# Four moves in the first third of a fused decoder layer: a gate tile ahead of attention, channel means behind a gate group, a weight split behind a convolution input, seven weight splits on another engine

## The chip, the cores and the metric

The kernel runs on one core of one Trainium2 chip. The metric is the device time of one execution in microseconds (us); the kernel before has a median of 1292.92 us over three runs (1291.68 to 1296.99). All positions below are us from the start of the span of the profiled execution. PE is TensorE, DVE is VectorE, ACT is ScalarE, POOL is GpSimd, SP is SyncE, which here only issues DMAs.

## The reference, cut to what matters

One layer over 1040 tokens (16 meta tokens in front of 1024), width 1024, all in float32:

```python
z = h @ w_in + b_in                       # 3840 columns: q | k | v | conv value, conv gate | two merge gates
a = swa_sink_attention(q, k, v, sinks, rel_bias)      # window 128, 8 heads, 16 meta keys, sinks
y_attn = a @ w_attn_proj
c = c_val * sigmoid(c_gate)
c = causal_dwconv(c, conv_dw, conv_dw_b)              # 31 taps, 512 channels
c = silu(layer_norm(c, conv_ln_g, conv_ln_b))         # mean and variance over the 512 channels
y_conv = c @ w_conv_proj
mixed = sigmoid(g_attn) * y_attn + sigmoid(g_conv) * y_conv
h = layer_norm(alpha * h + mixed @ w_out, ...)
h = layer_norm(alpha * h + conv_ffn(h), ...)
```

## The kernel before, in words

Every product of float32 matrices is made of three products in a reduced type (`fp32r`): each operand is split into a high and a low part, and high x high, high x low and low x high are summed in PSUM (`product`, lines 332, 335, 336). A weight tile of 1024 x 128 is loaded by SP (`weights`), its high part is a cast on ACT (`split`, line 300), and its low part a subtraction (line 303). That subtraction runs on DVE for the first 23 weight tiles of the kernel (the argument `n <= 23`) and on POOL for later ones. Two buffers each of the raw, high and low weights are in use, so that a tile's cast waits until PE has finished the tile two before it.

The input projection is worked through in tiles of 128 output columns, each over three groups of tokens (`z_tile`, `z_group`). One tile is 3 groups x 8 blocks x 3 matmuls, and each group has one of three PSUM banks until an evacuation has read it. The order of the tiles by count is: 1 to 3 the key tile, the value tile and the first query tile; 4 and 5 the gate and the value tile of convolution chunk 1 (`conv_chunk`); 6 and 7 those of chunk 0; 8 to 10 the other query tiles; 11 and 12 merge gates 0 and 1; 13 and 14 chunk 2; 15 to 17 gates 2 to 4; 18 and 19 chunk 3; 20 to 30 gates 5 to 15. So gate i has count 15 + i from gate 5 on. Weight tiles 31 to 38 belong to the projection of the two branches.

A convolution chunk leaves its input in `cin`, through three evacuations on DVE (line 697), one for each token group. The 31 taps (line 706) follow on DVE as 31 instructions for each of the four chunks, at a low rank, so that they fill DVE's time during attention. Behind chunk 3 the four chunks are summed into `csum`, two additions on POOL and the last (line 919) on DVE, and PE multiplies `csum` by a matrix of 1/512 to get the channel means (line 924), for three token groups.

Attention goes over eight blocks of 128 queries and two key groups: scores (lines 784 and 864), softmax on DVE and ACT, transposes, weighted values. Queries go out to DRAM (`qd`) and come back in another layout (`qt`), so that the first scores wait for that transfer.

The normalisation over channels, called the chain below, runs behind attention on DVE in an order written out by hand (`pin`): `cln_centre` (line 961), `cln_var` (line 971; sums over channels by PE, line 973), `cln_rstd` (lines 979 to 982), `cln_scale` (line 989, Silu on ACT, line 990), `cln_split` (lines 996, 997), and then `o_split` (lines 1008 to 1010), which scales the attention output and splits it. The last eight `o_split` calls serve token groups 1 and 2. The branch projection (`ps_p`) reads what `cln_split` and `o_split` write. The temporaries of the chain lie where attention had its tiles.

The order of instructions on each engine is set by a planner that simulates the kernel when it is built: among the instructions that are ready in its simulation it takes the one with the lowest rank (`rank`, `tc.cur_priority`). `after(x, y)` adds an edge to it: x is ordered behind y. On the chip each engine then runs its own list in order. Ranks that matter here: 500 for weight splits, 600 for evacuations, 30000 for attention, 38000 for the chain, 40000 for gate tiles, 60000 for taps, 70000 for the projection.

Of the kernel before, what the change touches and what calls it, by code (L numbers as in the profile page):

```python
# [26 lines left out]
OP = mybir.AluOpType  # L27
# [4 lines left out]
KC = D // P  # L32
# [78 lines left out]
def tile_hybrid_layer(  # L111
# [3 lines left out]
    nc = tc.nc  # L115
# [5 lines left out]
    def load(o, i):  # L121
        return nc.sync.dma_start(out=o, in_=i)

    def store(o, i):

        return nc.scalar.dma_start(out=o, in_=i)

    def f32(ap):
        return ap.bitcast(F)

    def after(ins, first):

        tc.add_manual_dep(ins.ins, first.ins.name, mybir.DependencyInfo(
            mybir.DependencyClass.NoSync, mybir.DependencyReason.SCHED_ONLY), reason="order of work")

    @contextmanager
    def rank(p):

        saved = tc.cur_priority
        tc.cur_priority = p  # L140
        yield
        tc.cur_priority = saved
# [35 lines left out]
    start = ExitStack()  # L178
# [45 lines left out]
    def bcol(m):  # L224
        return colA[:, m:m + 1]
# [10 lines left out]
    def ones_of(pool):  # L236
        t = pool.tile([P, P], F, name="ones", tag="ones", bufs=1)
        nc.vector.memset(t, 1.0 / CW)
        return t

    ones = ones_of(sp)
# [35 lines left out]
    def h0(k, hl, a, b):  # L277
        return (RHO, RHC)[hl][:, k * T + a:k * T + b]
# [17 lines left out]
    def wraw(shape):  # L296
        return wraw_p.tile(shape, F, name="wr", tag="wr")

    def split(raw, hi, lo, quick=False, behind=None):
        ins = nc.scalar.copy(hi, raw)  # L300
        if behind is not None:
            after(ins, behind)
        return (nc.vector if quick else nc.gpsimd).tensor_tensor(lo, raw, f32(hi), OP.subtract)  # L303

    def wsp(tag, dtype=R):
        return wsp_p.tile([P, KC, WS], dtype, name=tag, tag=tag)
# [1 line left out]
    def wsp_flat(tag, dtype=R):  # L308
        return wsp(tag, dtype).rearrange("p k c -> p (k c)")[:, W_FLAT:W_FLAT + D]

    fills = [0]
    last_fill, last_split = [], []

    def weights(shape, fill):
        fills[0] += 1
        n = fills[0]
        own = n == 3
        raw = OB[:, 0:D].rearrange("p (k c) -> p k c", k=KC) if own else wraw(shape)
        with rank({1: 14, 2: 13, 3: 16, 4: 23}.get(n, RK_SPLIT)):
            last_fill.append(fill(raw))  # L320
        hi, lo = ((sp.tile([P, KC, WS], R, name=t + "3") if own else wsp(t))[:, :, :P] for t in ("whi", "wlo"))
        if n <= 3:
            return hi, lo, raw
        with rank(RK_SPLIT):
            last_split.append(split(raw, hi, lo, n <= 23))
        return hi, lo

    def product(ps, terms, behind=None):

        n = len(terms)  # L330
        for i, (ah, al, bh, bl) in enumerate(terms):
            ins = nc.tensor.matmul(ps, ah, bh, start=i == 0, stop=False)  # L332
            if i == 0 and behind is not None:
                after(ins, behind)
            nc.tensor.matmul(ps, ah, bl, start=False, stop=False)  # L335
            last = nc.tensor.matmul(ps, al, bh, start=False, stop=i == n - 1)  # L336
        return last

    def z_group(wt, g, a, b, evac):
        hi, lo = wt  # L340
        ps = pat.tile([P, 512], F, name="ps_z", tag="mm", bufs=3)
        product(ps[:, :b - a], [(hi[:, k], lo[:, k], h0(k, 0, a, b), h0(k, 1, a, b)) for k in range(KC)])
        with rank(RK_EVAC):
            evac(g, a, b, ps[:, :b - a])

    def z_tile(fill, groups, evac, wt=None):
        wt = wt or weights([P, KC, P], fill)
        for g, (a, b) in enumerate(groups):
            z_group(wt, g, a, b, evac)

    def in_cols(m):
        return lambda raw: load(raw, w_z[m])

    TG = [(a + U0 if i == 0 else a, b) for i, (a, b) in enumerate(HG)]
# [3 lines left out]
    def stage(n, lo=4104, cnt=5):  # L358
        i = st_next[0] % cnt
        st_next[0] += 1  # L360
        return FA[:, lo + i * 400:lo + i * 400 + n]
# [158 lines left out]
    def span(i, g):  # L520
        a, b = HG[g]
        return (U0 if i == 2 and g == 0 else a), b
# [21 lines left out]
    def evac(g, *tiles):  # L544
        for i in tiles:
            a, b = span(i, g)
            with rank(RK_EVAC):
                evacs0[i](g, a, b, sums0[i])
# [92 lines left out]
    for a, b in ((0, 400), (400, J_LEN)):  # L641
        ps = pat.tile([P, 512], F, name="ps_v", tag="o" if a == 0 else "t", bufs=1 if a == 0 else 2)
# [17 lines left out]
    ones = ones_of(cp)  # L660
# [4 lines left out]
    Kx = [ap.tile([P, NB, 144], R, name=f"kx{g}") for g in range(NKV)]  # L665
# [17 lines left out]
    def conv_chunk(c):  # L683
        sig = {}

        def g_evac(g, a, b, ps):
            sig[g] = stage(b - a)

            nc.scalar.activation(sig[g], ps, AF.Tanh, bias=bcol(10 + c), scale=0.5)
            nc.scalar.activation(sig[g], sig[g], AF.Identity, bias=half_, scale=0.5)  # L690

        z_tile(in_cols(10 + c), HG, g_evac, wt_c1 if c == 1 else None)
        cin = cp.tile([P, 16 + T], F, name="cin", tag="cin")
        nc.vector.memset(cin[:, 0:16], 0.0)

        def v_evac2(g, a, b, ps):
            nc.vector.scalar_tensor_tensor(cin[:, 16 + a:16 + b], ps, bcol(6 + c), sig[g], OP.add, OP.mult)  # L697

        z_tile(in_cols(6 + c), HG, v_evac2)
        with rank(RK_CONV + c * 100):  # L700
            for j in range(TAPS):
                wc = cdw[:, j * CH + c:j * CH + c + 1]
                if j == 0:
                    nc.vector.tensor_scalar(acc[c], cin[:, j:j + U], wc, cdwb(c), OP.mult, OP.add)
                else:
                    nc.vector.scalar_tensor_tensor(acc[c], cin[:, j:j + U], wc, acc[c], OP.mult, OP.add)  # L706

    def gate_tile(i):
        b2, m = divmod(i, KC)

        def gate_evac(g, a, b, ps):
            t = stage(b - a)
            nc.scalar.activation(t, ps, AF.Tanh, bias=bcol(14 + i), scale=0.5)  # L713
            store(sgd[b2, m, :, a - U0:b - U0], t)

        z_tile(in_cols(14 + i), TG, gate_evac)

    for g in range(NKV):
        kr = FA[:, 2054 + g * T:2054 + (g + 1) * T]
# [24 lines left out]
    ps = pat.tile([P, 512], F, name="ps_vm", tag="t", bufs=2)  # L744
# [4 lines left out]
    for q4 in range(2):  # L749
        ps = pat.tile([P, 512], F, name="ps_v4", tag="t", bufs=2)  # L750
        for i in range(4):
            c = NMETA + (q4 * 4 + i) * P
            nc.tensor.transpose(ps[:, i * P:(i + 1) * P], vT[:, c:c + P], ident)
        src = ps[:, :].rearrange("p (n g d) -> p n g d", g=2, d=HD)
        for g in range(NKV):
            hi, lo = (V[:, q4 * 4:q4 * 4 + 4, g, i] for i in range(2))
# [10 lines left out]
    def load_q(g, i):  # L767

        n = P if i else P + 2
        t = ap.tile([P, 8 * (P + 2)], R, name="qt", tag="qt", bufs=3)[:, :8 * n]  # L770
        for h in range(2):
            load(f32(t[h * HD:(h + 1) * HD]), dram(qd, g * HD * 8 * U + q_at(i), [[8 * U, HD], [1, 8 * n]]))
        t = t.rearrange("p (l r q) -> p l r q", l=2, r=4)
        return t[:, 0], t[:, 1]

    tc.cur_priority = RK_ATT


    q0 = [load_q(g, 0) for g in range(NKV)]
    ps = pat.tile([P, 512], F, name="ps_s2", tag="t", bufs=2)  # L780
    for h in range(NH):
        g, r = divmod(h, 4)
        o = ps[:2, h * 16:(h + 1) * 16]
        nc.tensor.matmul(o, q0[g][0][:, r, 0:2], Kx[g][:, 0, 0:16], start=True, stop=False)
        nc.tensor.matmul(o, q0[g][1][:, r, 0:2], Kx[g][:, 0, 0:16], start=False, stop=True)
    s2 = ap.tile([2, NH, 16], F, name="s2")
    nc.vector.tensor_tensor(s2, ps[:2, :P].rearrange("p (h m) -> p h m", m=16), biasq, OP.add)
# [44 lines left out]
    ps = pat.tile([P, 512], F, name="ps_o", tag="o", bufs=1)  # L832
# [16 lines left out]
    for i in range(NB):  # L849
# [5 lines left out]
        for g in range(NKV):  # L855
# [6 lines left out]
            for r in range(4):  # L862
                ps = pat.tile([P, 512], F, name="ps_s", tag="s", bufs=2)
                nc.tensor.matmul(ps[:, :w], qh[:, r], keys, start=True, stop=False)
                nc.tensor.matmul(ps[:, :w], ql[:, r], keys, start=False, stop=True)
                h = g * 4 + r
# [18 lines left out]
            for c, kb in bands:  # L885
                ps = pat.tile([P, 512], F, name="ps_t", tag="t", bufs=2)
# [17 lines left out]
            weights_out(range({2: 0, 5: 3, 7: 6}[i], i + 1))  # L904

    tc.cur_priority = RK_Z
    order = list(range(0, 2)) + ["c2"] + list(range(2, 5)) + ["c3"] + list(range(5, 16))
    for o in order:
        if isinstance(o, str):
            conv_chunk(int(o[1]))  # L910
# [2 lines left out]
        if o == "c3":  # L913

            csum = cp.tile([P, 16 + T], F, name="csum", tag="cin")[:, :U]
# [4 lines left out]
    means = {}  # L920
    for g, (a, b) in enumerate(UG):
        with rank(RK_EVAC):
            means[g] = pat.tile([P, 512], F, name="ps_m", tag="st"[g % 2], bufs=2)
            nc.tensor.matmul(means[g][:, :b - a], ones, csum[:, a:b], start=True, stop=True)
    att.close()
    qsp_stack.close()

# [9 lines left out]
    ones = ones_of(tmp_p)  # L937
# [158 lines left out]
    for m in range(KC):  # L1096
        hi, lo = weights([P, KC, P], lambda raw: load(raw, w_ab[m]))
# [37 lines left out]
        if m in (2, 3):  # L1135
            raw = (FA[:, 4112:5136], OB[:, 3072:4096])[m - 2]
# [343 lines left out]
    for c in range(FC):  # L1480
        V4, X, Z, Y = (pup.tile([P, 1024], F, name=n, tag=n) for n in ("pw", "px", "pz", "py"))
        passes = ((1,), (0,)) if c == 0 else ((0, 1),)
        for subs in passes:
            last = subs == passes[-1]
            w_next = iter(range(7))
            a, b = SUB[subs[0]][0], SUB[subs[-1]][1]
# [54 lines left out]
            ins = tt(c22[:, a:b], c22[:, a:b], u13[:, a:b], OP.add)  # L1541
# [239 lines left out]
```

## Time and profile before

| | |
|---|---|
| median of three runs | 1292.92 us (1291.68 to 1296.99) |
| the profiled execution, and its span | 1290.93 us, 1289.1 us |
| busy: PE, DVE, ACT, POOL | 98%, 84%, 45%, 5% of the span |
| mean granted TensorE clock | 0.995 |
| input projection, attention, gates on PE | up to 436.65 us |
| branch and output projection, then the up and the down stage | from 436.65 us on |

A row of the timeline or of the waits has the start, the duration, the engine, the line, the operation, the output and inputs with their shapes, a count, and in brackets the idle time before it and what ended that. A row of the windows has a stretch, its length, the busy time of each engine with the number of instructions, the granted clock (1.00 is full) and the share and rate of the DMA engines.

### The profile page before, as it was taken

What the parts mean: (1) busy time and instruction counts of PE and PEld (TensorE: products, weight loads), DVE (VectorE), ACT (ScalarE), POOL (GpSimd) and SP (SyncE); (2) the same over time, 40 slices, a digit from 0 to 9 for tenths busy, and PEclk for the clock granted to TensorE, in tenths of its full rate; (3) what the DMA queues carried; (4) which work ended last, traced back from release to release, by engine and by line L of the source; (5) the groups of instructions that cost most, each with busy time, mean ns of one, the idle gap of its engine ahead of it and who ended that gap; (6) DMA issues with size and microseconds to landing.
All of it is one profiled execution on the core that took longest, in us unless ns stands there. A gap on an engine that the chain in (4) does not pass through costs nothing.

```text
span 1289.1 us, 21679 instructions
## 1 busy us (share of the span) xinstructions
PE 1263.4 (98%) x8546; PEld 1189.8 (92%) x8546; DVE 1085.9 (84%) x1836; ACT 580.3 (45%) x1051; POOL 66.4 (5%) x35
## 2 busy tenths in 40 slices
PE   7999999999999999999999999999999999999997
PEld 7889999999989999788899999999999997888886
DVE  7888999999967777647899999989899886887697
ACT  5423234454547222344664554555545543536330
POOL 2100000001112222100000000000000000000000
PEclk9999999999999999999999999999999999999999
DMA  6274734334243665222235454453455556989722
GB/s 245 83 265 108 185 93 116 100 82 115 67 112 119 201 166 146 92 82 82 83 103 204 173 208 178 182 202 129 161 182 195 196 198 242 393 286 388 260 76 82
DMA packets 96297, 212.11 MB, mean 165 GB/s; under 512 B 11059, under 2 KB 36211, under 8 KB 95938
## 3 DMA queue, kind: packets, MB, share of 16 engines
q1 hardware_dynamic: 84426, 199.64, 46.2%
q10 hardware_dynamic: 11768, 11.08, 2.6%
q8 instruction: 67, 1.10, 0.4%
q14 instruction: 36, 0.29, 0.1%
HBM read 150.29 MB, written 62.70 MB: 165 GB/s over the span
## 4 chain that ended last, share of the span: by engine, by line
PE 80%; DVE 13%; DMA 4%; ACT 1%; issue 1%; SPq 1%; ACTq 0%; POOL 0%; DVEq 0%
PE px L1502 14%; PE py L1502 9%; PE ps_x L1627 9%; PE ps_z L1627 5%; PE ps_z L332 5%; PE ps_z L335 5%; PE ps_z L336 5%; PE pz L1502 5%; PE pw L1502 5%; DVE FA L706 4%; PE ps_p L336 2%; PE ps_p L335 2%; PE ps_p L332 2%; PE ps_w L332 2%; PE ps_w L336 2%; PE ps_w L335 2%
## 5 line engine op out<-in xcount | busy, mean ns | idle before, releaser
L332 PE MATMUL ps_z<-RHO,whi 128*128 128x384 f32 (+2 forms) x648 | 209.8, 324 | 2.6 <-DVE cin L697 2.6
L335 PE MATMUL ps_z<-RHC,whi 128*128 128x384 f32 (+2 forms) x648 | 210.1, 324 | 0.0
L336 PE MATMUL ps_z<-RHO,wlo 128*128 128x384 f32 (+2 forms) x648 | 209.5, 324 | 0.0
L706 DVE SCALAR_TENSOR_TENSOR FA<-cin,cdw,FA 128x1026 f32<-128x1026 f32 x120 | 154.9, 1305 | 0.1
L332 PEld LDWEIGHTS ps_z<-RHO,whi 128*128 128x128 f32 x648 | 122.5, 189 | 3.5 <-DVE cin L697 3.0
L336 PEld LDWEIGHTS ps_z<-RHO,wlo 128*128 128x128 f32 x648 | 122.3, 189 | 1.2 <-issue 0.3
L335 PEld LDWEIGHTS ps_z<-RHC,whi 128*128 128x128 f32 x648 | 122.6, 189 | 0.7
L300 ACT CAST whi<-wr 128x1024 fp32r<-128x1024 f32 x37 | 38.8, 1049 | 75.6 <-PE ps_z L335 58.4
L1324 DVE TENSOR_TENSOR RHO<-wr,RHO 128x512 fp32r<-128x512 f32 x94 | 64.0, 689 | 9.5 <-ACT RHO L1323 9.5
L1323 ACT CAST RHO<-wr 128x512 fp32r<-128x512 f32 x94 | 56.7, 619 | 25.8 <-DVE wr L1341 11.6
L1341 DVE TENSOR_TENSOR wr<-wr 128x512 f32<-128x512 f32 x88 | 60.6, 689 | 0.2
L303 POOL TENSOR_TENSOR wlo<-wr,whi 128x1024 fp32r<-128x1024 f32 x17 | 42.1, 2474 | 187.2 <-ACT whi L300 158.8
L1514 ACT COPY FA<-px 128x514 f32<-128x514 f32 (+2 forms) x23 | 13.1, 571 | 79.0 <-PE px L1502 79.0
L713 ACT ACTIVATE FA<-ps_z,colr 128x384 f32<-128x384 f32 (+1 forms) x48 | 26.0, 542 | 48.4 <-PE ps_z L336 46.4
L1502 PE MATMUL px<-OA,RHO 128*128 128x258 f32 x324 | 43.2, 282 | 0.0
L1429 ACT ACTIVATE FA<-OB,coll 128x512 f32<-128x512 f32 x44 | 35.9, 816 | 15.2 <-DVE OB L1510 15.2
L1502 PE MATMUL px<-OC,RHO 128*128 128x256 f32 x324 | 42.2, 280 | 0.0
L1502 PE MATMUL px<-RHC,RHO 128*128 128x258 f32 (+1 forms) x312 | 40.9, 280 | 0.4 <-ACT OB L1514 0.4
L1514 ACT COPY OB<-px 128x514 f32<-128x514 f32 (+2 forms) x46 | 26.1, 567 | 32.6 <-PE px L1502 32.6
L1502 PEld LDWEIGHTS px<-OA,RHO 128*128 128x128 f32 x324 | 40.5, 189 | 0.2 <-ACT OB L1514 0.2
L880 ACT ACTIVATE s<-s,sm 128x272 f32<-128x272 f32 (+1 forms) x64 | 31.8, 500 | 18.1 <-DVE sm L876 16.3
L1502 PEld LDWEIGHTS px<-OC,RHO 128*128 128x128 f32 x324 | 39.9, 189 | 0.1
(468 smaller groups left out, 3387.2 us busy)
## 6 DMA issues: line engine op xcount, KB each, us to landing
wr<-in_w_up_dram SPq DMA_DIRECT2D x44, 512.0 KB, 4.2
wr<-in_w_z_dram SPq DMA_DIRECT2D x29, 512.0 KB, 4.0
fd<-FA SPq DMA_DIRECT2D x44, 256.0 KB, 2.5
OB<-in_w_down_dram SPq DMA_DIRECT2D x21, 512.0 KB, 4.7
FA<-sd SPq DMA_DIRECT2D x15, 512.0 KB, 8.1
qt<-qd SPq DMA_DIRECT2D x28, 256.0 KB, 4.0
sgd<-FA ACTq DMA_DIRECT2D x32, 192.0 KB, 2.6
td<-OB SPq DMA_DIRECT2D x12, 512.0 KB, 3.2
```

Of the source, the lines that this page charges most:

```text
L300: ins = nc.scalar.copy(hi, raw)
L303: return (nc.vector if quick else nc.gpsimd).tensor_tensor(lo, raw, f32(hi), OP.subtract)
L332: ins = nc.tensor.matmul(ps, ah, bh, start=i == 0, stop=False)
L335: nc.tensor.matmul(ps, ah, bl, start=False, stop=False)
L336: last = nc.tensor.matmul(ps, al, bh, start=False, stop=i == n - 1)
L706: nc.vector.scalar_tensor_tensor(acc[c], cin[:, j:j + U], wc, acc[c], OP.mult, OP.add)
L1323: nc.scalar.copy(hi, src)
L1324: ins = nc.vector.tensor_tensor(lo, src, f32(hi), OP.subtract)
L1341: ins = nc.vector.tensor_tensor(*x)
L1502: ins = nc.tensor.matmul(o, x[:, ks], bmat(sub, q, hl, k), start=first and k + j == 0, stop=k == 3 and j == 2, skip_group_check=not first)
L1514: copied.append(nc.scalar.copy(*x))
L1627: nc.tensor.matmul(banks[i], l[:, ts], r[:, ws], start=first and a and x + k == 0, stop=z and x == len(ops) - 1 and k == 2, skip_group_che ...
```

## The change

Four edits, none of which adds or removes arithmetic:

1. Gate tile 0 is written ahead of attention instead of behind it, and attention's first matmul is ordered behind the last matmul of that tile.
2. The three channel-mean products are ordered behind the first token group of gate tile 12.
3. The low part of weight tile 7 (the value tile of chunk 0) is ordered behind the last evacuation into the convolution input of chunk 1. Both run on DVE.
4. The low parts of weight tiles 24 to 30 (gates 9 to 15) are made on DVE instead of POOL.

To name these points, `z_group` and `z_tile` return their last matmuls.

```diff
-    fills = [0]
+    fills, cin_done, gate_mm = [0], [], {}
...
-            last_split.append(split(raw, hi, lo, n <= 23))
+            last_split.append(split(raw, hi, lo, n <= 30))
+            if n == 7:
+                after(last_split[-1], cin_done[-1])
...
-        product(ps[:, :b - a], [(hi[:, k], lo[:, k], h0(k, 0, a, b), h0(k, 1, a, b)) for k in range(KC)])
+        last = product(ps[:, :b - a], [(hi[:, k], lo[:, k], h0(k, 0, a, b), h0(k, 1, a, b)) for k in range(KC)])
         with rank(RK_EVAC):
             evac(g, a, b, ps[:, :b - a])
+        return last
...
-        for g, (a, b) in enumerate(groups):
-            z_group(wt, g, a, b, evac)
+        return [z_group(wt, g, a, b, evac) for g, (a, b) in enumerate(groups)]
...
-            nc.vector.scalar_tensor_tensor(cin[:, 16 + a:16 + b], ps, bcol(6 + c), sig[g], OP.add, OP.mult)
+            cin_done.append(nc.vector.scalar_tensor_tensor(cin[:, 16 + a:16 + b], ps, bcol(6 + c), sig[g],
+                                                           OP.add, OP.mult))
...
-        z_tile(in_cols(14 + i), TG, gate_evac)
+        gate_mm[i] = z_tile(in_cols(14 + i), TG, gate_evac)
...
+    gate_tile(0)
     tc.cur_priority = RK_ATT
...
-        nc.tensor.matmul(o, q0[g][0][:, r, 0:2], Kx[g][:, 0, 0:16], start=True, stop=False)
+        ins = nc.tensor.matmul(o, q0[g][0][:, r, 0:2], Kx[g][:, 0, 0:16], start=True, stop=False)
+        if h == 0:
+            after(ins, gate_mm[0][-1])
...
-    order = list(range(0, 2)) + ["c2"] + list(range(2, 5)) + ["c3"] + list(range(5, 16))
+    order = [1, "c2"] + list(range(2, 5)) + ["c3"] + list(range(5, 16))
...
-            nc.tensor.matmul(means[g][:, :b - a], ones, csum[:, a:b], start=True, stop=True)
+            ins = nc.tensor.matmul(means[g][:, :b - a], ones, csum[:, a:b], start=True, stop=True)
+            after(ins, gate_mm[12][0])
```

## The prediction, before the run

> **What bounds the kernel now.** I read the page first: who is busy, and who makes up the chain that ended last.
>
> ```profile
> span 1289.1 us, 21679 instructions
> PE 1263.4 (98%) x8546; PEld 1189.8 (92%) x8546; DVE 1085.9 (84%) x1836; ACT 580.3 (45%) x1051; POOL 66.4 (5%) x35
> ```
>
> PE is busy for 98% of the span, so the time is PE's work plus its holes. No edit removes PE work; the change can only close holes or open new ones. So the second view is the list of waits, for PE alone.
>
> ```profile
> PE ps_z L332 <- DVE cin L697: 2.6, 1, 2.6
> PE ps_s L784 <- DMA qt<-qd: 1.5, 2, 1.1
> PE ps_m L924 <- DVE csum L919: 1.4, 1, 1.4
> ```
>
> Three of the four edits name exactly these places: tile 7's low weights the first, the gate tile the second, the means the third. The third view is the timeline around each.
>
> **Edit 3, the first hole.**
>
> ```profile
> 86.61 1.04 ACT L300 CAST whi<-wr 128x1024 fp32r<-128x1024 f32 x1 [10.62 <-PE ps_z L335]
> 87.69 1.23 DVE L303 TENSOR_TENSOR wlo<-wr,whi 128x1024 fp32r<-128x1024 f32 x1 [4.98 <-ACT whi L300]
> 88.83 1.55 DVE L697 SCALAR_TENSOR_TENSOR cin<-ps_z,colr,FA 128x272 f32<-128x272 f32 x3
> 89.38 0.59 PE L332 MATMUL ps_z<-RHO,whi 128*128 128x272 f32 x1 [2.63 <-DVE cin L697]
> 94.00 0.34 PE L332 MATMUL ps_z<-RHO,whi 128*128 128x384 f32 x1
> 62.44 0.29 PE L332 MATMUL ps_z<-RHO,whi 128*128 128x272 f32 x1
> 65.44 0.34 PE L332 MATMUL ps_z<-RHO,whi 128*128 128x384 f32 x1
> 90.00:91.00 1.00, 1.00 (x6) 1.00 (x6) 1.00 (x3) 0.00 (x0) 0.00 (x0) 0.50 0.80 266
> ```
>
> Tile 7's split stood 4.98 us at the head of DVE's queue for its cast, which waited for a buffer that PE was still reading. All three evacuations of the chunk before stood behind it, and PE needed their banks: 2.63 us of hole. The hole cost more than its length. The windows row shows the granted clock at 0.50 behind it, and the 24 matmuls from 89.38 to 94.00 took 4.62 us where the same 24 from 62.44 to 65.44 took 3.00. With the split behind the evacuations, two of these run in DVE's idle time and the third as the tile ends. The split itself then starts when its cast is done, as before, and tile 7's matmuls begin over 10 us after that (tile 6, which takes 11, comes first). Nothing else is late. Gain: 2.63 + 1.62 = 4.25 us.
>
> The Trainium skill (TensorE: Matmul & The Clock Gate, Part 1) lets the clock fall only after an idle window of about 3.4 us. By it this hole would have cost 2.63 us alone, and the sum at the end would be 1.6 us less good. The trace disagrees: 2.63 us were enough for a clock of 0.50.
>
> **Edit 1, the second hole.**
>
> ```profile
> 137.65 0.28 PE L332 MATMUL ps_z<-RHO,whi 128*128 128x258 f32 x1
> 149.09 0.28 PE L332 MATMUL ps_z<-RHO,whi 128*128 128x258 f32 x1
> 153.81 0.17 PE L784 MATMUL ps_s<-kx,qt 128*2 128x16 f32 x1 [1.14 <-DMA qt<-qd]
> 155.96 0.17 PE L784 MATMUL ps_s<-kx,qt 128*2 128x16 f32 x1 [0.37 <-DMA qt<-qd]
> ```
>
> Gate 0 already begins at 149.09, ahead of attention; the scores cut into it and wait 1.14 + 0.37 = 1.51 us for queries. A tile takes 11.44 us (137.65 to 149.09). With gate 0 whole it ends at 149.09 + 11.44 - 4.25 = 156.3, after the queries have landed, so the 1.51 us are gained. The first of the two left the clock at 1.00 (first row of the next fence), so there is nothing more. The price is that all of attention waits 2.5 us longer (153.81 to 156.3), with its softmax on DVE and ACT behind it. DVE covers that with taps:
>
> ```profile
> 105.00:155.00 50.00, 35.48 (x29) 1.00 0.55 136
> 305.00:355.00 50.00, 30.63 (x23) 1.00 0.31 94
> ```
>
> These windows hold DVE's taps alone (busy time and count, then clock); there are taps to do from 105 until past 355, and gate tiles to do on PE beyond that. Without that cover the price would be 2.5 us. I take nothing.
>
> **Edit 2, the third hole.** The means wait 1.44 us for the last sum, with everything on PE behind them. Behind gate 12's first group that wait is gone: `csum` ends at 364.07, that group 20 us later. But the means then come late for DVE's chain, whose first step they are. What counts is how long the projection can do without the chain:
>
> ```profile
> 361.11 2.96 DVE L919 TENSOR_TENSOR csum<-csum,FA 128x1026 f32<-128x1026 f32 x1
> 364.13 1.35 PE L924 MATMUL ps_m<-csum,ones 128*128 128x386 f32 x4 [1.44 <-DVE csum L919]
> 365.31 1.95 DVE L961 TENSOR_TENSOR FA<-FA,ps_m 128x386 f32<-128x386 f32 x4
> 369.86 0.81 PE L924 MATMUL ps_m<-csum,ones 128*128 128x384 f32 x2
> 379.98 2.16 DVE L971 TENSOR_TENSOR t<-t 128x386 f32<-128x386 f32 x3 [0.28 <-ACT t L970]
> 393.49 0.34 PE L332 MATMUL ps_z<-RHO,whi 128*128 128x384 f32 x1
> 432.74 0.56 DVE L1010 TENSOR_TENSOR OA<-OB,OA 128x384 fp32r<-128x384 f32 x1
> 436.65 0.28 PE L332 MATMUL ps_p<-OA,whi 128*128 128x258 f32 x1
> 440.60 0.28 PE L332 MATMUL ps_p<-OA,whi 128*128 128x256 f32 x1
> ```
>
> In the kernel before, the early means are of no use to the chain after its first step: centring runs from 365.31, but the variance waits until 379.98, since its temporaries lie on attention's tiles. The slack at the end: the last split of token group 1 is done at 433.30, and PE reads it first at 440.60 (fourth block of the projection's second group). That is 7.3 us; the other groups have more.
>
> Now the chain after. Gate 12's first group ends at 393.49 before. Take off the three holes, 4.25 + 1.51 + 1.44 = 7.20 us, and what PE did ahead of that point and now does behind it: the means (about 2.0) and two variance sums, 0.8 each by the 0.81 row. That leaves 393.49 - 7.20 - 3.6 = 382.7. The first mean takes 0.8, centring two groups 2 x 1.95, so the variance starts at 387.4 instead of 379.98: 7.4 us later by the clock, though all of PE is 7.2 earlier.
>
> **Edit 4, POOL to DVE.**
>
> ```profile
> L303 DVE TENSOR_TENSOR wlo<-wr,whi x20: 1192/1218/1226, 55.3 to 315.6; 128x1024 fp32r<-128x1024 f32 x20
> L303 POOL TENSOR_TENSOR wlo<-wr,whi x17: 2386/2406/3467, 329.8 to 533.3; 128x1024 fp32r<-128x1024 f32 x17
> 346.21 3.47 POOL L303 TENSOR_TENSOR wlo<-wr,whi 128x1024 fp32r<-128x1024 f32 x1 [14.04 <-ACT whi L300]
> 347.33 2.44 DVE L803 TENSOR_TENSOR pm<-s,pm 128x64 f32<-128x64 f32 x1
> 407.52 2.41 POOL L303 TENSOR_TENSOR wlo<-wr,whi 128x1024 fp32r<-128x1024 f32 x1 [10.93 <-ACT whi L300]
> 407.54 3.69 DVE L989 TENSOR_TENSOR FA<-FA,t 128x256 f32<-128x256 f32 x4
> 414.99 2.42 POOL L303 TENSOR_TENSOR wlo<-wr,whi 128x1024 fp32r<-128x1024 f32 x1 [5.05 <-ACT whi L300]
> 415.18 2.44 DVE L1009 CAST OA<-OB 128x386 fp32r<-128x386 f32 x1
> 418.73 0.36 DVE L1009 CAST OA<-OB 128x386 fp32r<-128x386 f32 x1
> 437.85 2.40 POOL L303 TENSOR_TENSOR wlo<-wr,whi 128x1024 fp32r<-128x1024 f32 x1 [8.87 <-ACT whi L300]
> DVE wlo L303 <- ACT whi L300: 10.7, 5, 5.0
> ```
>
> It looks like 7 x 1.22 = 8.5 us more for a DVE that has no room. But a DVE instruction that starts beside a POOL split stands until it is over: the cast at 415.18 took 2.44 us, the same cast at 418.73 took 0.36; a 128x64 subtraction took 2.44. So POOL's splits already cost DVE about 2 us where they hit. Inside the chain two go away (407.52: 3.69 for four that should take some 1.4; 414.99: 2.1), 4.4 us in all. In their place come the DVE splits of tiles 29 and 30 at 1.2 each, of which one should fall into a wait for ACT: +1.2 (ends 0 and 2.4). Each also waits for its cast at the head of DVE's queue; the nearest row for that is the 4.98 at 87.69, the other end is nothing, and I take nothing, as 5 of the 20 DVE splits waited at all (last row). The first three moved splits lie ahead of `csum`, which has 20 us of room. Last, tile 32's split stays on POOL: at 437.85 it came just behind the chain's end; PE being 7.2 earlier and the chain later, it falls inside: +2.2 (ends 0 and 2.2).
>
> The Trainium skill (Perfetto Trace Analysis, Optimizing Scalar/DVE Operations) says that moving work between GpSimd and VectorE might not help, since they share a port. By it edit 4 would be worth nothing, and the sum would be 3.2 us worse. The trace agrees on the sharing (the two casts) but gives the move a gain inside the chain.
>
> **The sum.** The chain's end moves by S = 7.4 - 4.4 + 1.2 + 2.2 = 6.4 us. PE wants it 7.2 earlier and has 7.3 of slack, so PE waits 6.4 + 7.2 - 7.3 = 6.3 us in the projection, and the net is -7.2 + 6.3 = -0.9 us. If the planner sees that wait, it can put the convolution half of the second group in front of it, 12 matmuls of 0.12 us (33 of them lie between 436.65 and 440.60), 1.4 us; PSUM has one bank for that, not more. I take it, since the planner orders by readiness: -2.3 us (ends 0 and 2.8 for this term). Against the profiled execution (1290.93, span 1289.1) that is 1288.6; its time is 2.0 below the median shown, so the median becomes 1292.9 - 2.3 = 1290.6 us.
>
> **The rivals.** *All of the gain stays.* If the chain is shorter than I think, -7.2: 1285.7 us. It has waits to give, as the window of DVE's busy time over the chain shows:
>
> ```profile
> 379.00:438.00 59.00, 48.82 (x98) 1.00 0.53 150
> ```
>
> That is 10.2 us of waiting, and over 4 us of the busy time were blocked instructions. S must fall under 0.1. For it: the planner makes a new order for ACT, on which DVE waits there. Against: DVE's pinned order stays, and ACT's work is the same.
>
> *Slower: the chain is the bound.* One mechanism: the late means. If no wait shrinks, both new splits cost DVE and one waits for its cast as at 87.69, S = 6.4 + 1.2 + 5.0 = 12.6, and the net is 12.6 - 7.3 = +5.3. If a hole reaches 2.63 us, the clock falls and adds 1.6: +6.9, 1299.8 us. It decides from S = 7.3 on.
>
> *The change does not do what it says.* Gate 0 is already first; if the planner's new order only moves the holes (its simulation put tile 7's split before its cast), the time stays at 1293.
>
> **How the numbers follow.** Most of it paid back (-5 to +2): 0.50; all kept: 0.22; slower: 0.22; holes moved: 0.06. What a measurement can tell is about 0.5%, or 6.5 us. All kept lies just beyond it, so about two thirds of it counts as faster: 0.15. Of the slower case, with orders of the planner I can't foresee, three quarters lie beyond: 0.16. The range goes from the kept gain to the slower end: 1285.5 to 1299.5; the likeliest case alone is 1288 to 1295.
>
> **What would show it.** Right: no wait on `cin`, `qt` or `csum` in PE's list; clock 1.00 from 80 to 100; gate 12's first group ends near 383, the means right behind it; variance from about 387; POOL's first split of a weight is tile 31. PE waits at the first projection group for `OA`, some 5 us in pieces. Wrong: no such wait (gain kept), one piece of over 2.6 us with the clock at 0.50, or DVE standing for a cast in front of the chain.

## The result, and the profile after

The changed kernel takes 1290.64 us (median of 20 runs, 1288.21 to 1291.79) against 1294.37 us for the kernel before on the same chip (20 runs, 1290.98 to 1296.99). The ratio is 0.9971, with an interval of 0.9963 to 0.9979: 3.7 us faster. The median forecast was 1290.6 us, from a gain of 2.3. The profiled spans are 1289.1 and 1287.0 us.

The list of waits of PE in the changed kernel, without those that both kernels have at the start and in the last stages:

```profile
PE ps_z L334 <- ACT FA L716: 2.0, 1, 2.0
PE ps_p L337 <- DVE OA L1017: 1.9, 1, 1.9
```

The three waits on `cin`, `qt` and `csum` are gone and two others have come. The second, at the projection, had been forecast in kind, but as 6.3 us less 1.4. The first had not: PE waits for a bank that ACT has not emptied (the gate's evacuation, line 716 now). These are the places on PE's timeline, the means and the first scores among them:

```profile
62.95 0.29 PE L334 MATMUL ps_z<-RHO,whi 128*128 128x272 f32 x1
156.59 0.17 PE L788 MATMUL ps_s<-kx,qt 128*2 128x16 f32 x1
381.58 1.89 PE L930 MATMUL ps_m<-csum,ones 128*128 128x386 f32 x6
414.11 0.45 PE L334 MATMUL ps_z<-RHO,whi 128*128 128x384 f32 x1 [2.01 <-ACT FA L716]
419.96 0.28 PE L334 MATMUL ps_z<-RHO,whi 128*128 128x258 f32 x1
431.39 0.28 PE L334 MATMUL ps_p<-OA,whi 128*128 128x258 f32 x1
432.12 0.28 PE L334 MATMUL ps_p<-OA,whi 128*128 128x258 f32 x1
432.24 0.28 PE L334 MATMUL ps_p<-OC,whi 128*128 128x258 f32 x1
435.49 0.39 PE L337 MATMUL ps_p<-OA,whi 128*128 128x258 f32 x1 [1.90 <-DVE OA L1017]
```

The projection starts at 431.39 instead of 436.65. Counted from the first matmul of weight tile 4 (62.95 here, 62.44 before), so that the start of each execution does not come in, it starts 5.8 us earlier. The rows at 432.12 and 432.24 show the planner's new order: the attention half (`OA`) and the convolution half (`OC`) of a group alternate. The clock, by windows, at the old hole and behind the new one (the column behind POOL's):

```profile
86.00:90.00 4.00, 4.00 (x32) 4.00 (x31) 2.42 (x4) 1.05 (x1) 0.00 (x0) 1.00 0.71 279
414.00:418.00 4.00, 3.89 (x14) 3.89 (x15) 3.83 (x9) 1.60 (x4) 0.00 (x0) 0.59 0.66 165
```

The old hole is filled. Behind the new one the clock falls to a mean of 0.59 over four microseconds, and the 24 matmuls from 414.11 to 419.96 take 5.85 us, where half of the 48 of this shape between two tiles take some 4.2 (the gate tile's 11.44 us hold 24 of 258 columns, 3.0, and 48 of 384). So this hole cost 2.0 + 1.6 us in this execution. With the 1.9 at the projection, 5.5 us are paid back.

On DVE, the chain's first and last steps and what held it up, with POOL beside it:

```profile
386.16 1.88 DVE L978 TENSOR_TENSOR t<-t 128x386 f32<-128x386 f32 x3
392.76 1.23 DVE L303 TENSOR_TENSOR wlo<-wr,whi 128x1024 fp32r<-128x1024 f32 x1 [1.60 <-ACT whi L300]
413.61 1.23 DVE L303 TENSOR_TENSOR wlo<-wr,whi 128x1024 fp32r<-128x1024 f32 x1 [3.49 <-ACT whi L300]
432.54 2.47 POOL L303 TENSOR_TENSOR wlo<-wr,whi 128x1024 fp32r<-128x1024 f32 x1 [8.47 <-ACT whi L300]
432.83 2.61 DVE L1017 TENSOR_TENSOR OA<-OB,OA 128x386 fp32r<-128x386 f32 x1
442.07 0.56 DVE L1017 TENSOR_TENSOR OA<-OB,OA 128x384 fp32r<-128x384 f32 x1
```

The variance starts at 386.16 (387.4 was forecast) and the last split of token group 1 ends at 442.63: the chain's end moved by 9.3 us, not 6.4. Both splits that fall into the chain stood for their casts, tile 29's for 1.60 us and tile 30's for 3.49. Tile 32's split on POOL held the last low part of token group 0 for 2 us, and it is this instruction that PE waited for. ACT shows why both the cast and the evacuation were late:

```profile
408.25 1.28 ACT L985 ACT_TABLE_LOAD   x1
409.55 0.47 ACT L985 ACTIVATE t<-ps_m,eps 128x256 f32<-128x256 f32 x1
410.04 1.28 ACT L997 ACT_TABLE_LOAD   x1
411.34 1.31 ACT L997 ACTIVATE FA<-FA,colr 128x384 f32<-128x384 f32 x2
412.55 1.03 ACT L300 CAST whi<-wr 128x1024 fp32r<-128x1024 f32 x1
413.49 0.57 ACT L716 ACTIVATE FA<-ps_z,colr 128x384 f32<-128x384 f32 x1
```

These six rows fill 408.25 to 414.06 without a gap. PE reaches its next group at about 412.1 and needs the bank that the last row empties. It is behind two table loads of 1.28 us, a root and two Silu steps of the chain, and the cast.

### The profile page after: what moved, and what is told of

It is laid out like the page before. It is cut to its first block, busy times and chain, and to the rows that moved or that the text cites. A ratio compares the mean times of both kernels' runs of the same rounds, so it can differ in the third digit from the quotient of the medians.

```text
span 1287.0 us, 21685 instructions
## 1 busy us (share of the span) xinstructions
PE 1263.6 (98%) x8546; PEld 1191.0 (93%) x8546; DVE 1083.7 (84%) x1843; ACT 582.9 (45%) x1053; POOL 49.8 (4%) x28
## 4 chain that ended last, share of the span: by engine, by line
PE 88%; DVE 6%; DMA 2%; ACT 2%; issue 1%; SPq 0%; POOL 0%; DVEq 0%; ACTq 0%
PE px L1509 14%; PE py L1509 9%; PE ps_x L1634 9%; PE ps_z L334 7%; PE ps_z L337 7%; PE ps_z L338 7%; PE ps_z L1634 5%; PE pz L1509 5%; PE pw L1509 5%; PE ps_w L338 2%; PE ps_w L334 2%; PE ps_w L337 2%; PE ps_p L338 2%; PE ps_p L334 2%; PE ps_p L337 2%; DVE RHC L509 1%
## 5 line engine op out<-in xcount | busy, mean ns | idle before, releaser
L303 DVE TENSOR_TENSOR wlo<-wr,whi 128x1024 fp32r<-128x1024 f32 x27 | 32.8, 1216 | 14.5 <-ACT whi L300 14.4
L1509 PEld LDWEIGHTS px<-RHC,RHO 128*128 128x128 f32 x312 | 38.5, 189 | 0.7 <-ACT OB L1521 0.7
```

The source lines that it names most:

```text
L1509: ins = nc.tensor.matmul(o, x[:, ks], bmat(sub, q, hl, k), start=first and k + j == 0, stop=k == 3 and j == 2, skip_group_check=not first)
```

## The experiments

Two questions were open. Is each edit worth what its own hole cost? And do the late means set the payback, or ACT's and DVE's order, or POOL? Twelve kernels were run: each edit alone, the changed kernel without one edit, and the means at other places. All are compared with the kernel before on the same chip, whose median was 1293.94 to 1294.86 us.

### Each edit alone

The kernel before, with edit 3 alone:

```diff
             last_split.append(split(raw, hi, lo, n <= 23))
+            if n == 7:
+                after(last_split[-1], cin_done[-1])
```

> The kernel before with edit 3 alone (tile 7's low weights behind the evacuations). My theory: the hole at 87 goes with its slow clock, 4.25 us, and all later work moves with it, since the projection had 7.3 us of slack: about -4.2 us. Rival, that a hole costs only its idle time: -2.6 us. Rival, that a new order by the planner opens another hole: 0.

1289.89 us, ratio 0.9969 (0.9958 to 0.998), some 4.0 us faster. The profiles show the same size:

```profile
64.19 0.29 PE L334 MATMUL ps_z<-RHO,whi 128*128 128x272 f32 x1
434.16 0.28 PE L334 MATMUL ps_p<-OA,whi 128*128 128x258 f32 x1
```

From the first matmul of tile 4 to the first of the projection it is 369.97 us, and 374.21 in the kernel before (62.44 to 436.65): 4.24 us less, although the wait for queries is 2.1 us here for 1.5. With edit 2 alone:

```diff
-            nc.tensor.matmul(means[g][:, :b - a], ones, csum[:, a:b], start=True, stop=True)
+            ins = nc.tensor.matmul(means[g][:, :b - a], ones, csum[:, a:b], start=True, stop=True)
+            after(ins, gate_mm[12][0])
```

> The kernel before with edit 2 alone (means behind gate 12's first group). My theory: the wait for the last sum goes (-1.44), but the chain starts some 12 us later in absolute time less the 4.6 us that it had to wait for attention anyway, its splits stay on POOL, and the projection waits: +2 to +6 us net. Rival, that the chain has idle time to give: -1.4 us.

1299.19 us, ratio 1.0038 (1.0024 to 1.0052), 4.9 us slower. Its list of waits has two new holes as in the changed kernel, for ACT and in the projection, beside the two old ones that the edit does not touch. The wait on `csum` is gone, but one of the same length in attention has come in its place:

```profile
PE ps_z L332 <- DVE cin L697: 2.6, 1, 2.6
PE ps_z L332 <- ACT FA L714: 2.0, 1, 2.0
PE ps_s L785 <- DMA qt<-qd: 1.9, 1, 1.9
PE ps_pm L809 <- DVE pl L893: 1.4, 1, 1.4
PE ps_p L332 <- DVE OA L1011: 1.2, 1, 1.2
```

So edit 2 alone is enough to bring both new holes, at lines 714 and 1011 there. With edit 4 alone:

```diff
-            last_split.append(split(raw, hi, lo, n <= 23))
+            last_split.append(split(raw, hi, lo, n <= 30))
```

> The kernel before with edit 4 alone (seven low parts on DVE). My theory: DVE gains about 1.5 us net before the sum and 3 in the chain, none of which PE can use except at the wait for the last sum, which is at most 1.4: between 0 and -1.4 us. Rival, that DVE stands for casts as at tile 7 and the last sum comes later: +1 to +4 us.

1292.09 us, ratio 0.9986 (0.9977 to 0.9995), 1.8 us faster; the wait for `csum` is gone from its list. But the wait for queries is 2.2 us there for 1.5, and a wait for ACT's gate evacuation has come:

```profile
PE ps_z L332 <- ACT FA L714: 0.9, 1, 0.9
```

So in its profiled execution PE stands no less than before, and where the 1.8 us come from is not shown. With edit 1 alone:

```diff
+    gate_tile(0)
     tc.cur_priority = RK_ATT
...
+        if h == 0:
+            after(ins, gate_mm[0][-1])
...
-    order = list(range(0, 2)) + ["c2"] + list(range(2, 5)) + ["c3"] + list(range(5, 16))
+    order = [1, "c2"] + list(range(2, 5)) + ["c3"] + list(range(5, 16))
```

> The kernel before with edit 1 alone (gate tile 0 whole, then attention). My theory: -1.5 us, the two waits for queries. Rival, that attention's later start reaches the last sum, for which PE waits: up to +2.5 us, net +1.

1292.29 us, ratio 0.9988 (0.9979 to 0.9997), 1.6 us faster, but not only by the two waits for queries. These are gone from its list, and so is the wait on `csum`, for the last sum now ends at 356.6. In their place stands a wait for ACT's gate evacuation, with the clock at 0.50 behind it:

```profile
PE ps_z L332 <- ACT FA L714: 2.4, 1, 2.4
408.00:409.00 1.00, 1.00 (x4) 1.00 (x5) 1.00 (x1) 1.00 (x3) 1.00 (x1) 0.50 0.46 169
```

The means run from 356.6 in this kernel, so this wait does not need late means. The theory held for all four in sign. Edit 3 has the size of its hole by its mechanism; that edit 1 has it too is a coincidence. Edits 1, 3 and 4 alone add up to 7.4 us, with edit 2 to 2.5.

### The changed kernel without one edit

> The changed kernel without edit 2 (means as early as the planner likes). My theory: the last sum is done at 352, so PE hardly waits for it even without edit 2, the chain starts early: 2 to 6 us faster than the changed kernel, 1284.5 to 1288.5. Rival, that edit 2 is needed for the gain: slower than the changed kernel by the 1.4 us of the old wait, 1292.

Without `after(ins, gate_mm[12][0])` the time is 1284.06 us, ratio 0.9919 (0.9906 to 0.9931): 10.5 us faster than before, and 6.7 faster than the changed kernel. The edge is not needed for the third hole. This kernel is the one before with edits 1, 3 and 4: together they are worth 10.5 us, where alone they add up to 7.4 (a difference just beyond the intervals), and the waits for ACT that edits 1 and 4 bring alone are not in its list. Edit 2 on top of them costs 6.7 us. In the changed kernel the last sum is done at 351.6, 12 us earlier than before:

```profile
L925 DVE TENSOR_TENSOR csum<-csum,FA x1: 1199/1199/1199, 350.4 to 350.4; 128x1026 f32<-128x1026 f32 x1
```

It takes 1.20 us, and took 2.96 with a POOL split beside it. In this run the means ran from 356.2 on, and PE has no wait for the sum.

> The changed kernel without edit 4 (the seven low parts on POOL again). My theory: two more POOL splits block DVE inside the chain for some 2 us each, DVE saves 1.2 to 2.4 of its own splits and the 3.5 us in which it stood for a cast: 0 to +3 us against the changed kernel. Rival, that DVE's standing for casts is what the chain lacks: 2 to 3 us faster.

With the limit at 23 again, 1287.83 us, ratio 0.9952 (0.9939 to 0.9964): 2.5 us faster than the changed kernel by the two ratios. The time went the rival's way, though the two intervals just touch (0.9964 and 0.9963). That DVE's standing for casts is the cause was not shown: both new holes are still in the list, 2.0 us for ACT and 1.2 at the projection instead of 1.9, and POOL still holds a DVE instruction there for 2 us (2.42 us at 433.73). The next group has the same edit with early means.

### The means at other places, and POOL's last splits

```diff
-            after(ins, gate_mm[12][0])
+            after(ins, gate_mm[11][0])
```

> The changed kernel with the means behind gate 11's first group instead of gate 12's, one tile (11.4 us) earlier. My theory (late means set the chain, the chain sets the new holes): centring is done before attention frees the temporaries, the variance starts when these are free, some 6 us earlier than 386, the hole at the first projection group goes and perhaps the one at 412: 2 to 5 us faster than the changed kernel, 1285.5 to 1288.5. Rival, that the holes come from ACT's order and POOL's splits and not from the means: no faster than the changed kernel, 1290.5.

1282.33 us, ratio 0.9904 (0.989 to 0.9918), 12.4 us faster than before and 8.7 faster than the changed kernel. Both holes are gone:

```profile
63.89 0.29 PE L334 MATMUL ps_z<-RHO,whi 128*128 128x272 f32 x1
369.67 1.24 PE L930 MATMUL ps_m<-csum,ones 128*128 128x386 f32 x4
379.38 1.89 DVE L978 TENSOR_TENSOR t<-t 128x386 f32<-128x386 f32 x3 [0.28 <-ACT t L977]
400.00:440.00 40.00, 40.00 (x274) 40.00 (x273) 37.01 (x84) 14.24 (x25) 5.17 (x2) 1.00 0.66 202
428.62 0.28 PE L334 MATMUL ps_p<-OA,whi 128*128 128x258 f32 x1
```

The variance starts at 379.38, as in the kernel before, PE is busy for all of 400 to 440, and the projection begins 8.0 us earlier than before. This execution was 1.45 us later at tile 4 already (63.89 for 62.44), so from there it is 364.73 us for 374.21. These 9.5 us are what the holes were worth in the profiled execution.

> The changed kernel with the means behind gate 10's first group, one more tile earlier (ends about 354, the last sum about 352). My theory: the chain can't use earlier means, since the temporaries come free only at 377: level with gate 11, 1282 to 1283.5. Rival, that earlier is better still: -2 us. The other way: PE waits for the sum and the time rises by 1 to 2 us.

1283.28 us, ratio 0.9919 (0.9905 to 0.9932): level with gate 11 within the intervals, as expected. The variance starts at 380.41 there, no earlier than with gate 11, so the means can't be used earlier.

> Means behind gate 11, the seven low parts on POOL again. My theory: with slack in the chain edit 4 is worth little; POOL's splits block DVE for 2 us each and may bring back a wait at the projection: 0 to +3 us against the kernel with means behind gate 11 (1282.3). Rival, that DVE standing for casts costs more, as the changed kernel without edit 4 hints: -1 to -3 us.

Means behind gate 11 and the limit at 23: 1287.91 us, ratio 0.9947 (0.9933 to 0.9962), 5.6 us slower than with edit 4. The price is again one wait for ACT, with a slower clock behind it:

```profile
404.69 0.45 PE L334 MATMUL ps_z<-RHO,whi 128*128 128x384 f32 x1 [2.17 <-ACT FA L716]
400.00:440.00 40.00, 37.83 (x239) 37.50 (x238) 35.42 (x73) 15.32 (x26) 10.04 (x4) 0.96 0.68 206
```

The means run at 370.85 here, so this is a second kernel in which the wait for ACT comes without late means. So edit 4 is worth 5.6 us with early means and costs 2.5 with late ones. With early means most of it is this wait, which came with another order of ACT's list, and not POOL's blocking of DVE.

> The changed kernel with two more low parts (weight tiles 31 and 32) on DVE. My theory: the DVE instruction that stood beside POOL for 2 us just ahead of the first projection group (2.61 us at 432.83) no longer does, the PE wait of 1.9 us there goes: -1 to -2 us against the changed kernel. Rival, that the wait is set by the chain's length anyway: 0 to +2.4 us, two more splits of 1.2.

The changed kernel with the limit at 32: 1291.36 us, ratio 0.998 (0.9971 to 0.9989), not faster than the changed kernel. The wait that was to go came back larger elsewhere in the projection, and the wait of 2.0 us for ACT stayed:

```profile
PE ps_p L334 <- DVE OB L1122: 3.6, 1, 3.6
```

> Means behind gate 11 and the low parts of tiles 31 and 32 on DVE too. My theory: PE has no hole left in this stretch, so there is nothing to gain: 0, at most +1 us against 1282.3. Rival, that POOL's blocking still costs: -1 to -2 us.

1283.39 us, ratio 0.9916 (0.9902 to 0.9929): level, as expected. POOL's blocking of DVE costs nothing where PE has slack.

### The same late means without table loads

The chain's root and Silu on ACT were replaced by functions that need no table load: there is none from 376 to 430, where the changed kernel has eight. The normalisation's values are changed by that. The instructions are otherwise the same, and PE, DVE, ACT and POOL each run them in the same order as in the changed kernel.

```diff
-        nc.scalar.activation(r_, pv_, AF.Abs_reciprocal_sqrt, bias=eps, scale=1.0)
+        nc.scalar.activation(r_, pv_, AF.Square, bias=eps, scale=1.0)
...
-            nc.scalar.activation(y, y, AF.Silu, bias=clnb(c), scale=clng(c))
+            nc.scalar.activation(y, y, AF.Tanh, bias=clnb(c), scale=clng(c))
```

> The changed kernel with the chain's two functions on ACT replaced by ones that need no other table than the gates' (Square for the reciprocal root, Tanh for Silu): the normalisation's numbers are changed, no instruction is left out but the table loads. My theory: the hole of 2.0 us at 412 comes from eight table loads of 1.28 us that hold up a gate's evacuation, and the chain waits for the same loads: both new holes go, -5 to -8 us against the changed kernel, level with the kernel that has its means behind gate 11 (1282 to 1285). Rival, that the late means alone set the chain: the hole at 412 goes, but the wait at the projection stays: -2 to -4 us.

1282.0 us, ratio 0.9906 (0.9893 to 0.992): the late means stay, and the whole payback goes.

```profile
382.96 3.81 DVE L968 TENSOR_TENSOR FA<-FA,ps_m 128x386 f32<-128x386 f32 x8 [1.38 <-PE ps_m L930]
405.02 1.30 ACT L997 ACTIVATE FA<-FA,colr 128x384 f32<-128x384 f32 x2
406.22 1.04 ACT L300 CAST whi<-wr 128x1024 fp32r<-128x1024 f32 x1
407.15 0.58 ACT L716 ACTIVATE FA<-ps_z,colr 128x384 f32<-128x384 f32 x1
400.00:440.00 40.00, 40.00 (x275) 39.95 (x274) 36.90 (x84) 13.15 (x25) 5.43 (x2) 1.00 0.57 155
435.45 0.56 DVE L1017 TENSOR_TENSOR OA<-OB,OA 128x384 fp32r<-128x384 f32 x1
```

Centring starts at 382.96, as late as in the changed kernel, but the last split of group 1 ends at 436.0 instead of 442.6. PE has no hole from 400 to 440. The two Silu steps, the cast and the evacuation follow one another on ACT as in the changed kernel, and PE does not wait for them. So in this order the table loads make the payback, and the late means without them cost nothing.

The two new holes differ in what else they need. The wait for ACT does not need late means: it is 2.4 us with edit 1 alone and 2.2 with the means behind gate 11 and without edit 4. Table loads alone do not make it either: the kernel without edit 2 has eight of them between 385 and 405 and no wait for ACT. What decides is the order in which the planner puts ACT's list, and why it comes out one way or the other was not separated further. The wait for `OA` at the projection is there only in kernels with the means behind gate 12 (1.9 us in the changed kernel, 1.2 with edit 2 alone, 1.2 without edit 4), and it goes without the loads: it needs both.

## Why the prediction was right, and where it was not

**The gain.** Forecast 7.2 us for the three holes. With the means behind gate 11, where no new hole is in the way, it was 9.5 in the profiled execution and 12.4 by the medians. The sum left out a wait of 0.39 us in attention (at 203.32 before) and that the matmuls overlap: from 411.76 to 414.11 in the changed kernel it is 2.35 us from start to start, where 0.18 is usual, and the list calls this a hole of 2.01. Edit 3 was worth 4.0 for 4.25, so the slow clock behind the hole was rightly counted with it; idle time alone would have been 2.6. Edit 1 alone was worth 1.6 for 1.51, but by other terms: the third hole closed with it, and a wait for ACT opened. Attention's later start (156.59) cost nothing.

**Gate 12's first group** was to end at 382.7, and the means run at 381.58.

**The payback.** Forecast 4.9 us (6.3 less the planner's 1.4). The new holes with their clock are 5.5 in the profiled execution; by the medians the changed kernel is 8.7 slower than the one with means behind gate 11. Gain and payback both came out larger than forecast, so that the net fits as well as it does is in part luck. The place was not right either. The step that failed is the one where PE waits only in the projection, for the second group (the signs at the end of the prediction name the first group, and there it came). Two terms in it were wrong in opposite ways:

- The planner's filling was taken as one group of 12 matmuls, 1.4 us. It interleaved the two halves, matmul by matmul inside each group too, over the whole of the projection's start. Inside a group that takes no bank beyond the one that each half has anyway, so the limit of one bank did not bind. By the prediction's own sum, with the chain 9.3 us late, PE 5.3 early and 7.3 of slack, PE would have waited 7.3 us; it waited 1.9, and at the first group. So about 5.4 us were hidden.
- ACT was left out as a source of holes. Table loads, Silu, a cast and an evacuation follow one another there, and PE lost 2.0 us and 1.6 of clock at 412.

**The chain's move S** was 9.3 us for 6.4. Tile 32's POOL split fell inside it as forecast (2.61 us for an instruction of 0.56). The wait of the moved splits for their casts was taken as 0, with ends of 0 and 5; inside the chain it was 1.60 and 3.49. Without the table loads the same chain ends at 436.0, 2.7 us later than before and not 9.3.

**Edit 4** was counted as a gain of 3.2 us inside the chain. With the late means it was a loss of 2.5; with early ones a gain of 5.6. The blocking that it removes was read rightly (the last sum takes 1.20 us instead of 2.96), the price of DVE's standing for casts was not. With early means what decided was neither, but a wait of 2.2 us for ACT; with late ones the cause is open.

**The rivals.** "All of the gain stays" needed S under 0.1; with the means behind gate 11 it does stay, and the last split of group 1 ends at 427.5 there, 5.8 us earlier than before. The slower rival, late means as the bound, is what edit 2 does alone: 4.9 us slower, where its estimate was 5.3 for the whole change. The sizes agree by chance: the chain's end moved by 18.3 us there (to 451.6), not 12.6.

**The median** came out 0.04 us from the forecast, but the kernel before measured 1294.37 in 20 runs, not 1292.92, so the gain was 3.7 us and not 2.3. Part of this agreement is luck.

## What to carry to other kernels

A hole on PE costs its length and what the clock loses behind it, so close holes first and count both. Moving an early step of a chain to close one hole is safe only as far as the next thing that holds the chain anyway, here the temporaries. In the kernels whose first mean ran anywhere from 356 to 371, the variance started between 377.5 and 383.6; so one gate tile earlier than 12 was worth 8.7 us, and a second one nothing. Try an edit without its neighbours too: the third hole closed without edit 2, which on top of the other three cost 6.7 us. Before a chain is moved beside other work, read the lists of all engines that serve both; here ACT, busy 45% of the span, made the new hole, because functions with different tables, casts and evacuations met in one stretch. In seven of the thirteen changed kernels a wait for its gate evacuation appears that the kernel before does not have.

## What the runs showed of the hardware that was not expected

The fall of the clock behind a hole is not sure. The same wait on `cin`, 2.6 us by the list of each kernel, was followed by 0.50 in the kernel before, but not in the kernel with edit 1 alone; and a wait for queries of 2.1 us left the clock alone in the kernel with edit 3, where one of 2.2 us did not in the kernel with edit 4. The wait of 2.0 us for ACT cost clock in the changed kernel and none in the one without edit 4 (1.00 from 414 to 420). One window of each behind its hole, in the order edit 1, edit 3, edit 4:

```profile
92.00:94.00 2.00, 2.00 (x18) 2.00 (x18) 1.91 (x9) 0.00 (x0) 0.00 (x0) 1.00 1.14 407
```

```profile
154.00:156.00 2.00, 2.00 (x13) 2.00 (x13) 1.94 (x3) 0.00 (x0) 0.00 (x0) 1.00 1.01 357
```

```profile
158.00:160.00 2.00, 2.00 (x8) 2.00 (x7) 2.00 (x3) 0.00 (x0) 0.00 (x0) 0.50 0.67 220
```

A fall, once it comes, always cost the same. Over six microseconds around it the mean clock is 0.72 in the kernel before (88 to 94), in the changed kernel (414 to 420) and in those with edit 1 alone (406 to 412), with edit 4 alone (157 to 163) and with gate 11 without edit 4 (404 to 410). That is some 3.4 us at 0.50, or 1.7 us lost. The first two of these windows:

```profile
88.00:94.00 6.00, 4.62 (x24) 4.62 (x25) 5.67 (x17) 0.00 (x0) 0.00 (x0) 0.72 0.66 233
414.00:420.00 6.00, 5.89 (x25) 5.89 (x26) 5.79 (x14) 3.35 (x8) 0.00 (x0) 0.72 0.62 175
```

The Trainium skill (TensorE: Matmul & The Clock Gate, Part 1) describes the window in which activity is judged as free-running, 3.4 us long. That fits a fall by chance of position and the 3.4 us that a fall lasts, though not a threshold of a whole idle window: all of these holes are shorter. Falls by chance would also explain the spread: the kernel before ran from 1290.98 to 1296.99 us, the kernel with means behind gate 11, without these holes, from 1281.49 to 1282.94, and the medians differ by 12 us where the profiled spans differ by 8.0. The profiled execution of before was then one in which only one of the holes cost clock. The runs of the kernel before bear it out in part: of 47 with a recorded clock, the five at the lowest mean, 0.991, have a mean span of 1294.2 us, the two at the highest, 0.996, one of 1289.8. That this is the whole cause of the spread is argued and was not shown.
